# A hybrid decoder trunk on one core: the recurrence's banks are emptied right behind their products, and four due times are moved

## The chip, the cores and the metric

The kernel runs on one core of a Trainium2 chip, as one launch. The metric is the device time of that launch in microseconds (us), as the median of several runs. A profiled execution of the same program gives the trace from which all shorter times here are read. The engines are named as the profile names them: PE (TensorE, the matmuls; PEld its weight loads), DVE (VectorE), ACT (ScalarE), POOL (GpSimd) and SP (SyncE, which issues most DMAs).

## The reference

The program computes two decoder layers on x of 1024 tokens by 1024 columns, in float32. Layer 0 mixes tokens by a gated linear recurrence (HGRN2), layer 1 by sliding-window attention; each is followed by a gated convolution FFN. The change touches the recurrence and the way into layer 0's FFN:

```python
q, f, i, g = jnp.split(h @ w_in, 4, axis=-1)          # w_in: (1024, 4096), 8 heads of 128
fg = lb + (1.0 - lb) * jax.nn.sigmoid(heads(f))
o = hgrn2_chunkwise(jax.nn.silu(heads(q)), 1.0 - fg, heads(i), jnp.log(fg))
# S_t = diag(f_t) S_{t-1} + k_t v_t^T ; o_t = S_t^T q_t
o = o * lax.rsqrt(jnp.mean(jnp.square(o), -1, keepdims=True) + RMS_EPS)
o = o * g_norm_w * jax.nn.silu(heads(g))
mix = o.reshape(B, S, D) @ w_out
h = layer_norm(ALPHA * h + mix, ln_mix_g, ln_mix_b)
u = h @ ffn_w_in          # (1024, 5632), then conv of width 3, silu gate, @ ffn_w_out
```

## The kernel before, in words

**Matmuls.** Every large matmul is done to nearly float32 accuracy from operands split into a high part (cast on ACT) and a low part (the rest, subtracted on DVE: `low_part`, L197). `mm3` (L222 to L224) issues three matmuls of 128x128 by 128x512: high by high, high by low, low by high. Four such groups make a *product*, 12 matmuls.

**The recurrence's line of products.** The projections q, f (which makes the gates and keys), i (values) and g (output gate) are done head by head. Head 0's come first, in the plain way. For heads 1 to 7 the projections go in pairs: pair m = 2(h-1) is (f, q) of head h, pair m + 1 is (i, g). Each pair is done by seven products p = 1 to 7 on sums of blocks (a Strassen-Winograd scheme: the tokens' halves against the halves of the 1024 inputs). `line` lists the 98 products of all pairs in the order of PE: (m,1), (m-1,3), (m-1,4), (m,6), (m,5), (m,2), (m,7), and so on; the first pair has 1, 2, 6, 5, 7 in a row. The four x operands of these products are T, and TXs[0] to TXs[2] with the sums of x's blocks, made by `sums_of_x` and `last_sums`. The fourth product, (0,5), reads the last part of T that `last_sums` fills (cast L874, low part L197); the code finishes `last_sums` right before it.

**Banks.** The products share four PSUM banks (`product`, L1401). Product 2 has bank 1, products 5 and 3 have bank 2, and 1, 6, 7, 4 of pair m add up in bank 0 or 3, by m's parity. Product 6 adds onto what product 1 left, 7 onto 6, and 4 onto 7, so a product may not start before the bank's last content has been read. That reading is `evacuate` (L1367): a copy on ACT for products 1, 6, 5 and 4 (L1378 to L1387), an add on DVE for 2, 7 and 3 (L1390), and behind the add a gate on ACT (`forget`, L1013, or Silu). `readers[b]` holds the evacuation of bank b, so that the next product on b can see to it that it has been issued.

**Weights.** `job_next` (L1304 on) makes the products' weights in the order of `jobs`: sums "a" and "b" of a pair (two DVE operations each, L1315 and L1316, L1318 and L1319) and one low part per product (DVE, L197), behind a cast of the high part (`cast_next`, ACT, L1296). The low part of product 4 of a pair also issues the loads of two raw weight tiles for the pairs to come (SP). `ensure(n)` (L1356) forces these jobs until the product at place n of the line has its weights; `product(n)` calls it for n + 2. Weights lie in a ring of eight slots (`home`).

**The order.** Inside this stage PE, SP, ACT, DVE and POOL do their instructions in the order in which the code issues them. `Order` (L55) plans that order by hand: `od.t` is the planned time of PE, advanced with each matmul issued, and `od.v` the planned end of DVE's work, advanced by `od.vec`. A task (`od.spawn(gen, delay)`) is a generator that issues some instructions, yields the time until its next step is due, and is stepped by `od.tick()`, which is called behind each group of three matmuls. A tick steps the tasks that are due, then issues casts that are ready (`hook`), then fills DVE with jobs (`fill`) as long as `od.v` is less than 0.5 us ahead of `od.t`. `od.behind(us, least)` (L72) is the time until DVE's planned end plus `us`, and at least `least`. So an evacuation spawned with a delay of 0.3 was issued at the first tick of the next product: behind the `ensure` at that product's start and behind tasks due earlier.

**A head's recurrence.** `recur` (L1044 on) is a task too: elementwise products and updates on DVE (L1114 to L1119), copies of their results on ACT (`stash`, L1101, L1102), small matmuls of 32 rows for the sums and scores on PE (L228), and so on; near its end it turns the values' tile on PE (for heads from 1 on), copies it back on ACT (L1194), waits a due time of 1.3 us and multiplies keys by values (L228). `all_heads` does one head after the other and waits between them until the next head's gates are there. `values` (L753) empties a block of head 0's values and gates: copy (ACT, L756), add (DVE, L758), and behind every second block a Silu of two blocks (ACT, L765), due 0.7 us behind the add's issue.

**The entry of a layer.** `ffn` calls `out_proj` (L356 on): the mixer's output projection in two halves of the columns, eight token blocks each; in the second half the blocks come as 4, 5, 6, 7, 0, 1, 2, 3, and behind each block its `Up.ln` (L418) is spawned: the layer norm on DVE (`ln_affine`, L280, L283), and some us of matmuls later its turn: 8 transposes on PE (L232) into two banks of the same pool of four that `out_proj` uses, split into T by ACT and DVE. That due time was 10.0 for blocks 4 to 7 and 8.0 for blocks 0 to 3, in both layers. `Up.run` then does the up-projection by seven products of its own. Outside the recurrence and the attention only PE's order is the code's; the other engines are ordered by a scheduler, and the code between `urgent()` goes first.

Of the kernel before, what the change touches and what calls it, by code (L numbers as in the profile page):

```python
# [22 lines left out]
NH = 8  # L23
# [111 lines left out]
def trunk(ctx: ExitStack, tc: tile.TileContext, a: dict, out: bass.AP):  # L135
    nc = tc.nc
    PS = bass.MemoryType.PSUM
    od = Order()
# [29 lines left out]
    def psmm():  # L168
        return mmp.tile([P, 512], F32, name="psmm")

    def psax():
        return axp.tile([P, 1024], F32, name="psax")

    def urgent():

        return tc.high_priority(offset=300)
# [54 lines left out]
    def tr(ps, src):  # L231
        nc.tensor.transpose(ps, src, ident)  # L232
        od.t += 0.109
# [14 lines left out]
    def split(hi, lo, src, eng=None):  # L248
        nc.scalar.copy(hi, src)  # L249
        return low_part(lo, src, hi, eng)  # L250
# [8 lines left out]
    def ln_half(tb, i):  # L259

        if tb not in half_stats:
            half_stats[tb] = sm.tile([P, 2, 6], F32, name="st", bufs=8)
        nc.vector.bn_stats(half_stats[tb][:, i, :], Y[:, tb, i * 512:(i + 1) * 512])  # L263
# [10 lines left out]
    def ln_affine(tb, rows, dst, n=1):  # L274

        y = Y[:, tb, :]
        mv, rs = ln_stats(tb)
        parts = [slice(h * D // n, (h + 1) * D // n) for h in range(n)]
        for hs in parts:
            nc.vector.scalar_tensor_tensor(y[:, hs], y[:, hs], mv[:, 0:1], rows[0][:, hs],  # L280
                                           op0=ALU.subtract, op1=ALU.mult)
        for hs in parts:
            nc.vector.scalar_tensor_tensor(y[:, hs], y[:, hs], rs, rows[1][:, hs], op0=ALU.mult, op1=ALU.add)  # L283
            nc.sync.dma_start(dst(hs), y[:, hs])
# [118 lines left out]
    class Up:  # L403
# [14 lines left out]
        def ln(self, tb):  # L418
            with urgent():
                ln_affine(tb, self.rows, lambda hs: ynd[:, tb, hs], 2 if tb == 3 else 1)  # L420
            yield 10.0 if tb > 3 else 8.0
            turned = lambda t: (self.rx[2 * t - 4] if t in (2, 3) else Y[:, t, :]).rearrange("p (k t) -> p k t", k=KC)
            hf = turned(tb)
            ts = slice(tb * P, (tb + 1) * P)
            with urgent():
                for q in range(2):
                    ps, ks = psmm(), slice(4 * q, 4 * q + 4)
                    for k in range(4):
                        tr(ps[:, k * P:(k + 1) * P], Y[:, tb, (4 * q + k) * P:(4 * q + k + 1) * P])
                    pv = ps.rearrange("p (k t) -> p k t", k=4)  # L430
                    if tb < 4:
                        split(T[:, 0, ks, ts], T[:, 1, ks, ts], pv)
                        nc.scalar.copy(hf[:, ks], pv)
                    elif q == 0:
                        nc.scalar.copy(hf[:, ks], pv)
                    else:
                        split(T[:, 0, ks, ts], T[:, 1, ks, ts], pv)
                        tt(hf[:, ks], hf[:, :4], pv, op=add)
                        split(T[:, 0, :4, ts], T[:, 1, :4, ts], hf[:, ks])
                        return  # L440
            sf = turned(tb + 4)
            a11, a12, a21, s1 = hf[:, :4], hf[:, 4:], sf[:, :4], sf[:, 4:]
            tt(a21, a11, a21, op=sub)
            tt(a11, s1, a11, op=sub)
            tt(a12, a12, a11, op=sub)
            split(self.T2[:, 0, :, ts], self.T2[:, 1, :, ts], a21)
            yield 100.0
            pair = hf.rearrange("p (c k) t -> p c k t", c=2)
            split(self.TX[:, :, 0, :, ts], self.TX[:, :, 1, :, ts], pair)
# [37 lines left out]
        def product(self, p, fc, ps):  # L487
            TX = self.TX
            moving = {1: lambda j, k: T[:, j, k, :512], 2: lambda j, k: T[:, j, 4 + k, :512],
                      3: lambda j, k: TX[:, 1, j, k, :], 4: lambda j, k: T[:, j, 4 + k, 512:],  # L490
                      5: lambda j, k: T[:, j, k, 512:], 6: lambda j, k: TX[:, 0, j, k, :],
                      7: lambda j, k: self.T2[:, j, k, :]}[p]
            block = {1: 0, 2: 1, 5: 2, 4: 3, 7: 4, 6: 5, 3: 6}[p]
            ws = self.W[fc]
            fixed = lambda j, k: (ws[6][:, 512 * j + 128 * k:512 * j + 128 * k + 128] if block == 6 else
                                  ws[block // 2 * 2 + j][:, 512 * (block % 2) + 128 * k:512 * (block % 2) + 128 * k + 128])
            for k in range(4):
                mm3(ps, lambda j: fixed(j, k), lambda j: moving(j, k), k == 0, k == 3)
                od.tick()
            return ps  # L500
# [84 lines left out]
    class Down:  # L585
# [70 lines left out]
        def evacuate(self, p, tb, ps, ln):  # L656
            lo, hi = [Y[:, t, :].rearrange("p (h n) -> p h n", h=2) for t in (tb, tb + 4)]
            c11, c12, c21, c22 = lo[:, 0], lo[:, 1], hi[:, 0], hi[:, 1]
            plus, minus = {1: ([c11, c21], [c12, c22]), 2: ([c11], []), 5: ([c12, c22], []), 6: ([c21], [c22, c12]),
                           7: ([c22], [c21]), 3: ([c12], []), 4: ([c21], [])}[p]  # L660
            for y, op in [(y, add) for y in plus] + [(y, sub) for y in minus]:
                if p == 1:
                    nc.vector.scalar_tensor_tensor(y, y, ALPHA, ps, op0=ALU.mult, op1=op)
                else:
                    tt(y, y, ps, op=op)

            if p in (2, 3, 4, 7):
                ln_half(tb if p in (2, 3) else tb + 4, 0 if p in (2, 4) else 1)
            if p in (3, 4):
                task = ln(tb if p == 3 else tb + 4, self)  # L670
                if task is not None:
                    self.tasks.append(od.spawn(task))
# [51 lines left out]
    with tc.tile_pool(name="t", bufs=1, reuse_waits="tile") as raws, hgrn_pool as hp:  # L724
# [28 lines left out]
        def values(tb, ps):  # L753

            vg = VG[0][:, :, tb * P:(tb + 1) * P]
            nc.scalar.copy(vg, ps[:, 256:].rearrange("p (g c) -> p g c", g=2))  # L756
            yield 0.9
            nc.vector.tensor_tensor(vg, vg, ps[:, :256].rearrange("p (g c) -> p g c", g=2), op=ALU.add)  # L758
            od.vec(0.45)
            if tb == NB - 1:  # L760
                values_in[0] = 0
            if tb % 2:
                G = VG[0][:, 1, (tb - 1) * P:(tb + 1) * P]
                yield 0.7
                nc.scalar.activation(G, G, AF.Silu)  # L765

        def first_values(ps):
# [276 lines left out]
        def recur(h, qs, fg, kp):  # L1044
# [96 lines left out]
            ps = psax()  # L1141
# [37 lines left out]
            ps = psax()  # L1179
# [10 lines left out]
            if h:  # L1190
                ps = psax()
                for c in range(NB):
                    tr(ps[:, c * P:(c + 1) * P], V[:, c, :])
                nc.scalar.copy(VG[h][:, 0, :], ps)  # L1194
                yield 1.3
            ps = psax()
            for c in range(NB - 1):
                cs = slice(c * P, (c + 1) * P)
# [12 lines left out]
            ps = psax()  # L1211
# [45 lines left out]
        line = [(0, 1), (0, 2), (0, 6), (0, 5), (0, 7)]  # L1257
# [20 lines left out]
        def home(n):  # L1278
            return HL[:, n % 8, :].rearrange("p (h n) -> p h n", h=2)
# [76 lines left out]
        def ensure(n):  # L1356
            while line[n] not in low_made:
                if not job_next(True):
                    raise ValueError("a weight block is not made")
# [5 lines left out]
        targets, readers, evacs = {}, {}, {}  # L1365
# [35 lines left out]
        def product(n):  # L1401

            m, p = line[n]
            ensure(min(n + 2, len(line) - 1))
            b = {2: 1, 5: 2, 3: 2}.get(p, 3 * (m % 2))
            ps = banks[b]
            if b in readers:
                t, taken = readers[b]
                while not taken:
                    od.step(t)  # L1410
            w = home(n)
            for k in range(4):
                od.t += 0.031
                mm3(ps, lambda j: w[:, j, k * P:(k + 1) * P], lambda j: moving[p](j, k), k == 0 and p in (1, 2, 5), k == 3, onto=p in (6, 7, 3, 4))
                od.tick()
            done[0] = n + 1
            taken = []
            readers[b] = od.spawn(evacuate(m, p, ps, taken), 0.3), taken
            evacs.setdefault(m, []).append(readers[b][0])

        values_done, normed = [-1], []
        wo = a["hgrn_w_out"][0]
# [42 lines left out]
        with tc.manual_schedule(engines={EN.PE, EN.SP, EN.Activation, EN.DVE, EN.Pool}):  # L1465
# [27 lines left out]
            for n, (m, p) in enumerate(line):  # L1493
# [3 lines left out]
                h, g = pairs[m]  # L1497
# [55 lines left out]
        ps = psax()  # L1553
# [26 lines left out]
    with (tc.tile_pool(name="ta", bufs=1, reuse_waits="tile") as raws,  # L1580
# [190 lines left out]
        with tc.manual_schedule(engines={EN.PE, EN.Activation, EN.DVE, EN.Pool}):  # L1771
# [34 lines left out]
            for c in range(8):  # L1806
                fill = q_proj(hl) if c < 7 else last_filler()
                nq, nd = next(fill)
                for bp in range(0, 4, 2):
                    n = 2 * c + bp // 2  # L1810
# [49 lines left out]
            for _ in range(2):  # L1860
                ps = psax()
# [49 lines left out]
```

## Time and profile before

| | |
|---|---|
| median of 3 runs | 2125.34 us (2123.89 to 2126.57) |
| profiled execution, whole | 2124.68 us |
| profiled execution, span from first to last instruction | 2122.8 us |
| mean granted clock of TensorE | 0.997 |
| the line of 98 products | from 63.2 to about 442.5 us of the span |
| DVE busy, ACT busy | 84%, 45% of the span |

Lines of the profile name the engine, the line of the code, what is written and what is read. In a timeline the first two numbers are the start and the length in us, and a bracket at the end gives how long the engine stood idle before, and whose end it waited for. In the list of waits the numbers are the total in us, how many times, and the longest. In a table by stage, each engine has its busy time and its number of instructions; the last three numbers are the granted clock of TensorE, the busy share of the DMA engines, and GB/s.

### The profile page before, as it was taken

The page shows a single profiled execution, that of the slowest core. Times are in us where ns is not written, and L with a number is a line of the kernel's source. Part 1 is how long each engine was busy: PE and PEld are TensorE (multiplying, and loading weights), DVE is VectorE, ACT ScalarE, POOL GpSimd, SP SyncE. Part 2 cuts the span into 40 slices and gives each one's busy share as a digit, 9 for nine tenths or more (in the row PEclk, how much of TensorE's full clock was granted, in tenths as well). Part 3 has the DMA queues.
Part 4 walks back from the last instruction along what each step waited for, and adds up shares of the span by engine and source line. Part 5 has one row for each costly group of instructions (what it writes and reads, how often), then busy time and mean ns, then how long its engine had stood idle before and what let it go on. Part 6 is the DMA issues. An engine that isn't in the chain of part 4 may idle for free. (4 is left out here: it accounts for less than half of the span.)

```text
span 2122.8 us, 31567 instructions
## 1 busy us (share of the span) xinstructions
PE 2093.4 (99%) x12303; PEld 1740.8 (82%) x12303; DVE 1777.7 (84%) x2420; ACT 965.2 (45%) x1562; POOL 187.2 (9%) x214
## 2 busy tenths in 40 slices
PE   9899999999999999999999999999999999999998
PEld 8687888887888888888888888888888888888887
DVE  6677777768999999988988768969999999978986
ACT  6454555542444344434433267743544444444430
POOL 1000000001110000100001122321010000000002
PEclk9999999999999999999999999999999999999999
DMA  4011111253237766628854511042266776449662
GB/s 153 21 51 51 51 51 52 63 190 100 90 117 182 178 167 161 159 91 293 276 189 159 159 33 38 23 149 95 85 170 168 178 171 164 122 149 328 224 206 99
DMA packets 239823, 286.81 MB, mean 135 GB/s; under 512 B 30217, under 2 KB 160441, under 8 KB 239417
## 3 DMA queue, kind: packets, MB, share of 16 engines
q1 hardware_dynamic: 223360, 238.26, 34.7%
q0 software_dynamic: 15456, 46.16, 10.9%
q8 instruction: 97, 1.59, 0.3%
q14 instruction: 54, 0.43, 0.1%
q10 hardware_dynamic: 856, 0.37, 0.1%
HBM read 241.72 MB, written 89.15 MB: 156 GB/s over the span
## 5 line engine op out<-in xcount | busy, mean ns | idle before, releaser
L222 PE MATMUL psmm<-T,HL 128*128 128x512 f32 x816 | 323.1, 396 | 6.9 <-ACT T L874 3.6
L223 PE MATMUL psmm<-T,HL 128*128 128x512 f32 x816 | 319.0, 391 | 1.7 <-DVE T L197 1.7
L224 PE MATMUL psmm<-T,HL 128*128 128x512 f32 x816 | 319.2, 391 | 0.3 <-DVE HL L197 0.2
L528 DVE SCALAR_TENSOR_TENSOR Y<-Y,cwt,Y 128x1023 f32<-128x1023 f32 (+1 forms) x176 | 225.2, 1281 | 49.6 <-ACT Y L526 48.3
L249 ACT CAST HL<-rx 128x1024 fp32r<-128x1024 f32 (+1 forms) x151 | 150.8, 1005 | 149.8 <-DMA rx<-in_ffn_w_in_dram 33.1
L197 DVE TENSOR_TENSOR HL<-rx,HL 128x1024 fp32r<-128x1024 f32 (+1 forms) x151 | 180.1, 1198 | 14.9 <-ACT HL L249 14.5
L222 PEld LDWEIGHTS psmm<-T,HL 128*128 128x128 f32 x816 | 153.8, 188 | 38.9 <-ACT T L874 4.1
L224 PEld LDWEIGHTS psmm<-T,HL 128*128 128x128 f32 x816 | 153.7, 188 | 33.6 <-DVE HL L197 1.2
L223 PEld LDWEIGHTS psmm<-T,HL 128*128 128x128 f32 x816 | 153.9, 189 | 33.3 <-DVE T L197 2.7
L222 PE MATMUL psax<-T,HL 128*128 128x512 f32 x392 | 153.2, 391 | 1.3 <-DVE Y L513 0.9
L224 PE MATMUL psax<-T,HL 128*128 128x512 f32 x392 | 152.6, 389 | 0.0
L223 PE MATMUL psax<-T,HL 128*128 128x512 f32 x392 | 152.5, 389 | 0.0
L526 ACT ACTIVATE Y<-Y,cwt 128x1024 f32<-128x1024 f32 x88 | 108.8, 1237 | 91.9 <-DVE Y L515 80.5
L197 DVE TENSOR_TENSOR HL<-raw,HL 128x512 fp32r<-128x512 f32 (+1 forms) x121 | 92.7, 788 | 43.2 <-ACT HL L1296 33.5
L271 POOL TENSOR_TENSOR rs<-rs,nhalf 128x1 f32<-128x1 f32 x32 | 45.6, 1425 | 735.1 <-DVE rs L270 731.1
L249 ACT CAST HT<-rx 128x1024 fp32r<-128x1024 f32 (+1 forms) x37 | 35.5, 960 | 146.1 <-DVE rx L482 62.0
L222 PEld LDWEIGHTS psax<-T,HL 128*128 128x128 f32 x392 | 73.6, 188 | 17.6 <-DVE Y L513 1.3
L222 PE MATMUL psmm<-HL 128*128 128x512 f32 x220 | 86.5, 393 | 0.0
L224 PEld LDWEIGHTS psax<-T,HL 128*128 128x128 f32 x392 | 73.6, 188 | 15.4
L223 PEld LDWEIGHTS psax<-T,HL 128*128 128x128 f32 x392 | 73.6, 188 | 15.0
L224 PE MATMUL psmm<-HL 128*128 128x512 f32 x220 | 85.7, 390 | 0.0
L223 PE MATMUL psmm<-HL 128*128 128x512 f32 x220 | 85.6, 389 | 0.0
(404 smaller groups left out, 5197.1 us busy)
## 6 DMA issues: line engine op xcount, KB each, us to landing
rx<-in_ffn_w_in_dram SPq DMA_DIRECT2D x136, 256.0 KB
rx<-gd SPq DMA_DIRECT2D x118, 256.0 KB
bsd<-in_ffn_w_out_dram POOLq DMA_DIRECT2D x36, 768.0 KB, 8.6
gd<-Y SPq DMA_DIRECT2D x44, 512.0 KB
raw<-in_hgrn_w_in_dram SPq DMA_DIRECT2D x30, 512.0 KB
rx<-in_ffn_w_out_dram SPq DMA_DIRECT2D x54, 256.0 KB
R<-bsd SPq DMA_DIRECT2D x44, 256.0 KB
Y<-in_ffn_w_in_dram SPq DMA_DIRECT2D x40, 256.0 KB
```

The costliest lines, as they stand in the source:

```text
L197: make = lambda e: e.tensor_tensor(lo, src, hi.bitcast(F32), op=ALU.subtract)
L222: nc.tensor.matmul(ps, st(0), mv(0), start=start, stop=False, skip_group_check=onto)
L223: nc.tensor.matmul(ps, st(0), mv(1), start=False, stop=False, skip_group_check=onto)
L224: nc.tensor.matmul(ps, st(1), mv(0), start=False, stop=stop, skip_group_check=onto)
L249: nc.scalar.copy(hi, src)
L271: nc.gpsimd.tensor_tensor(rs, rs, nhalf, op=ALU.pow)
L526: nc.scalar.activation(c, u, AF.Identity, bias=cwt[:, l, 3, ci:ci + 1], scale=cwt[:, l, 2, ci:ci + 1])
L528: nc.vector.scalar_tensor_tensor(c[:, sh:], u[:, :S - sh], cwt[:, l, 2 - sh, ci:ci + 1], c[:, sh:], op0=ALU.mult, op1=ALU.add)
```

## The change

Five edits. (1) `product` steps the evacuation's task itself, as soon as the product's matmuls have been issued, so that its first instruction (copy or add) is issued there; it is no longer issued at the first tick of the next product. (2) `product(n)` asks for the weights of product n + 3, not n + 2. (3) The Silu of head 0's gates in `values` is due 0.1 us behind DVE's planned end, and at least 0.7. (4) In `recur`, the products of keys by values are due 2.2 us behind the copy of the turned values, not 1.3, for heads 1 to 5; heads 6 and 7 keep 1.3. (5) In layer 0, the turns of blocks 4 to 7 are due 13.0 us behind their layer norm, not 10.0; blocks 0 to 3 keep 8.0, and layer 1 keeps 10.0 and 8.0. No instruction is added or left out.

```diff
@@ -418,7 +418,7 @@
         def ln(self, tb):
             with urgent():
                 ln_affine(tb, self.rows, lambda hs: ynd[:, tb, hs], 2 if tb == 3 else 1)
-            yield 10.0 if tb > 3 else 8.0
+            yield 8.0 if tb < 4 else 10.0 if self.l else 13.0
@@ -761,7 +761,7 @@
             if tb % 2:
                 G = VG[0][:, 1, (tb - 1) * P:(tb + 1) * P]
-                yield 0.7
+                yield od.behind(0.1, 0.7)
                 nc.scalar.activation(G, G, AF.Silu)
@@ -1192,7 +1192,7 @@
                 nc.scalar.copy(VG[h][:, 0, :], ps)
-                yield 1.3
+                yield 2.2 if h < NH - 2 else 1.3
@@ -1401,7 +1401,7 @@
             m, p = line[n]
-            ensure(min(n + 2, len(line) - 1))
+            ensure(min(n + 3, len(line) - 1))
@@ -1415,8 +1415,9 @@
             done[0] = n + 1
             taken = []
-            readers[b] = od.spawn(evacuate(m, p, ps, taken), 0.3), taken
+            readers[b] = od.spawn(evacuate(m, p, ps, taken)), taken
             evacs.setdefault(m, []).append(readers[b][0])
+            od.step(readers[b][0])
```

## Prediction, made before the changed kernel was run

> **What bounds the kernel now.** I read the page first, then PE's waits, then timelines around the longest of them, then the table by stage.
>
> ```profile
> span 2122.8 us, 31567 instructions
> PE 2093.4 (99%) x12303; PEld 1740.8 (82%) x12303; DVE 1777.7 (84%) x2420; ACT 965.2 (45%) x1562; POOL 187.2 (9%) x214
> ```
>
> PE sets the time: it is idle for about 29 us of 2122.8. No arithmetic is taken away by this change, so all it can win is idle time of PE, or time at a lower clock. The profiled execution took 2124.68 us, 1.9 us more than its span and 0.7 us less than the median of the runs, 2125.34. Next: who keeps PE waiting, from 60 to 480 us (us in total, times, longest), and two rows of the same view over 0 to 620 us.
>
> ```profile
> PE psmm L222 <- ACT T L874: 3.6, 1, 3.6
> PE psmm L222 <- DVE VG L1390: 2.8, 1, 2.8
> PE psax L228 <- ACT VG L1194: 2.6, 5, 0.7
> PE psmm L222 <- ACT fg L1378: 1.8, 1, 1.8
> PE psmm L223 <- DVE T L197: 0.9, 1, 0.9
> ...
> PE psmm L232 <- DVE Y L283: 2.0, 1, 2.0
> PE psmm L224 <- DVE HL L197: 0.2, 1, 0.2
> ```
>
> Together 13.9 us, and each of these waits stands where the change has an edit. A row understates its loss: a matmul of 512 columns is shown busy for 0.39 us, but the next one starts 0.23 us behind it, so each wait costs 0.16 us more than its idle time.
>
> **Evacuation first, at 188 us.** The add that empties bank 2 is L1390; DVE, then PE:
>
> ```profile
> 184.70 0.71 DVE L1318 TENSOR_TENSOR raw<-raw 128x512 f32<-128x512 f32 x1
> 185.44 0.69 DVE L1319 TENSOR_TENSOR raw<-raw,raw 128x512 f32<-128x512 f32 x1
> 186.82 0.69 DVE L197 TENSOR_TENSOR HL<-raw,HL 128x512 fp32r<-128x512 f32 x1 [0.68 <-ACT HL L1296]
> 187.43 0.68 DVE L1390 TENSOR_TENSOR VG<-VG,psmm 128x512 f32<-128x512 f32 x1
> ```
>
> ```profile
> 185.06 0.39 PE L224 MATMUL psmm<-Y,HL 128*128 128x512 f32 x1
> 188.25 0.47 PE L222 MATMUL psmm<-T,HL 128*128 128x512 f32 x1 [2.81 <-DVE VG L1390]
> ```
>
> PE could have gone on at 185.06 + 0.23 = 185.29 and went on at 188.25: 2.96 us lost. Ahead of the add stand the two sums and the low part that ensure() forces, and DVE's own 0.68 us wait for the cast between them. These are issued in the next product, ahead of the evacuation, whose task is due 0.3 us later. The change issues the evacuation as soon as its product's matmuls are issued, so the add starts where the first sum did, 184.70, and ends at 185.4: PE waits 0.1 to 0.2 us, a gain of 2.8. Three products ahead, the sums are also forced a product earlier, which may push the recurrence's step that DVE did before them behind the add; then all 2.96 go. I take **2.8** (2.3 if DVE lags by another operation, to 2.96).
>
> The edit adds no instruction. Where an engine reaches the evacuation before PE has finished the product, what is queued behind it waits too: forced sums and low parts on DVE, casts on ACT, and the products that use them. They are for products two or three later, at 2.72 us each (12 matmuls of 0.23), which covers it; without cover a product would lose at most one low part and one cast, 0.69 us and a quarter of 2.17 (a row below). I take 0.
>
> **Weights three products ahead.** The same sums and low parts, 2.72 us earlier; two weight loads on SP behind the low part of product 4 go ahead with it, and their tiles still wait for the last cast that reads them. The wait at a low part (0.2 idle, 0.36 lost) goes: **0.3**. Against it, up to four DVE operations (two sums, two low parts, 4 x 0.6 us at the pace above) now stand ahead of an update of the recurrence that they used to follow. Its consumer, PE's small matmuls, is issued at DVE's planned end plus 0.6 us, so it moves back by whole matmul groups (0.68 us) instead of waiting; heads 2 to 5 wait for the next head's gates, so there it costs nothing.
>
> **Values' gate later, and the first products.** ACT, then PE:
>
> ```profile
> 63.51 0.42 ACT L765 ACTIVATE VG<-VG 128x256 f32<-128x256 f32 x1 [5.96 <-DVE VG L758]
> 63.83 0.35 ACT L756 COPY VG<-psmm 128x256 f32<-128x256 f32 x1
> ...
> 68.09 2.17 ACT L1296 CAST HL<-raw 128x512 fp32r<-128x512 f32 x4
> 70.17 0.58 ACT L1378 COPY fg<-psmm 128x512 f32<-128x512 f32 x1
> ```
>
> ```profile
> 68.56 0.39 PE L224 MATMUL psmm<-T,HL 128*128 128x512 f32 x1
> 70.80 0.50 PE L222 MATMUL psmm<-Y,HL 128*128 128x512 f32 x1 [1.85 <-ACT fg L1378]
> ...
> 77.51 0.39 PE L224 MATMUL psmm<-Y,HL 128*128 128x512 f32 x1
> 81.53 0.79 PE L222 MATMUL psmm<-T,HL 128*128 128x512 f32 x1 [3.64 <-ACT T L874]
> 83.18 0.79 PE L223 MATMUL psmm<-T,HL 128*128 128x512 f32 x1 [0.86 <-DVE T L197]
> ```
>
> The gate at 63.51 held ACT for 5.96 us, with the next block's copy (63.83) behind it; DVE in turn waited for that copy. With the gate due behind DVE's planned end, the copy is done long before, and the chain copy, add, update, ACT's copies, last gate and casts up to the evacuation at 70.17 comes about 0.8 us earlier. The evacuation keeps its place there, since no other ACT work was issued between. So the third product starts at about 70.0 instead of 70.80.
>
> The fourth product waits for the last quarter of x's sums in T. Its chain starts when the recurrence's scores leave PE:
>
> ```profile
> 76.38 0.69 DVE L1114 TENSOR_TENSOR qp<-qp,tot 128x512 f32<-128x512 f32 x1 [4.31 <-PE psax L228]
> ...
> 81.22 1.91 DVE L197 TENSOR_TENSOR T<-VG,T 128x512 fp32r<-128x512 f32 x3
> ```
>
> From 76.38 to the last low part's end, 83.13, are 6.75 us that the change leaves as they are. (The evacuation of the third product, 0.58 us on ACT, now stands ahead of the last cast; that delays the fourth product's first matmul, not the second, which waits for DVE.) But the scores move back by one group of three matmuls, 0.68 us, since a low part is forced ahead of the update before them. At equal clock 0.8 - 0.7 leaves nothing. The clock decides (PEclk is the column behind the engines):
>
> ```profile
> 67.92:71.33 3.41, 1.56 (x7) 1.01 (x6) 2.47 (x5) 3.35 (x7) 0.00 (x0) 1.00 0.00 0
> 71.33:74.74 3.41, 3.41 (x25) 1.98 (x27) 0.74 (x2) 0.00 (x0) 0.00 (x0) 0.50 0.00 0
> ...
> 81.57:88.40 6.83, 5.97 (x13) 4.37 (x14) 2.76 (x5) 0.51 (x2) 0.00 (x0) 0.50 0.46 131
> 183.97:187.38 3.41, 1.48 (x7) 0.90 (x5) 2.65 (x5) 1.21 (x3) 0.00 (x0) 1.00 0.00 0
> ```
>
> In the stretch behind the 1.85 us wait the granted clock is 0.50 for 3.41 us, behind the next for 6.83 us. Half of 3.41 is 1.7 us lost. With the wait cut from 2.01 lost (70.80 - 68.56 - 0.23) to 1.2, PE is busy for over half of the 3.41 us, and I expect full clock; then the scores leave 1.7 + 0.1 = 1.8 us earlier, and so does the fourth product. The second spell stays, as the wait before it gets longer (about 6 us); it may end a stretch earlier. I take **2.0** for both; bounds -0.3 (spell stays, one group later) and 3.5 (both shorten by a stretch). The Trainium skill ("TensorE: Matmul & The Clock Gate", "Why this matters for your kernels") asks for idle gaps of over some 3 us before the clock halves. The trace disagrees: 1.85 us was enough here, while 2.81 us at 188 left the clock at 1.00. By that rule the shorter gap would change no clock and this term would be about 0, the time 2 us longer.
>
> **Products later behind the values' turns.**
>
> ```profile
> 151.85 0.39 PE L224 MATMUL psmm<-T,HL 128*128 128x512 f32 x1
> ...
> 152.95 0.41 PEld L228 LDWEIGHTS psax<-VG,kd 128*128 128x128 f32 x3 [1.13 <-ACT VG L1194]
> ```
>
> PE comes to the values 0.87 us too early here, while ACT copies the turned values (152.95 - 151.85 - 0.23). Five such waits make 2.6 + 5 x 0.16 = 3.4. With 2.2 for 1.3, and issue points every 0.68 us, two more groups (1.36 us) lie between, which covers 0.87 with 0.5 to spare, for heads 1 to 5, all five. If a forced cast stands ahead of the copy on ACT, up to 0.6 comes back in some. I take **3.2** (2.3 to 3.4).
>
> **First entry's turns later.**
>
> ```profile
> 516.71 1.09 PE L232 MATMUL psmm<-ident,Y 128*128 128x128 f32 x8 [1.99 <-DVE Y L283]
> ```
>
> ```profile
> 500.00:573.00 73.00, 71.01 (x344) 58.70 (x344) 70.61 (x109) 31.14 (x48) 11.80 (x8) 1.00 0.27 96
> ```
>
> 3 us of matmuls more ahead of the first turn cover the 2.15 us lost. But DVE is busy 70.61 of 73 us there, so PE's lead can be given back where PE next waits for DVE. And block 0 comes one product (24 matmuls, 5.4 us) behind block 7: its turn, due after 8, stood 3 us behind block 7's, due after 10; with 13 they meet in one product, so four turned halves and the running product want five banks of a pool of four; the last waits for an ACT copy or a DVE operation, 0.6 to 1.3 us by the rows above. I take **1.2** (-0.5 to 2.15).
>
> **The sum.** 2.8 + 0.3 + 2.0 + 3.2 + 1.2 = 9.5; 0.5 off for small waits that a new order of 98 products brings somewhere, the size of the smallest rows above. 2124.7 - 9.0 = 2115.7, and with the 0.7 us by which the median stood higher 2116.4. All good ends make 12.3 (2113), all bad ones with 3 us of new waits 1.1 (2124).
>
> **Rivals.** *The gains of the first products and of the first entry don't come* (clock stays at 0.50, DVE takes back the turns): for it, DVE's 70.61 of 73 and the spells that I can't date; 2.8 + 0.3 + 3.2 - 0.5 = 5.8, so 2119.6 (2118.4 if the clock alone stays). By the Trainium skill's rule above that last case is the likely one; the row of 0.50 behind 1.85 us speaks against it, and I leave it a third of this rival's chance. *The waits move on*: a bank or a cast is late elsewhere by 0.7 us or so per head, 5 us over seven, against a gain of 5 to 9; 2121 to 2125, no change. For it, DVE was 3 us behind PE at 188; against it, DVE stands idle for a sixth of the span. *Slower*: the forced group of four (2.4 us) stands ahead of the update in each of seven heads, and PE reaches the scores before it, because real DVE lags its plan by more than the 0.6 us margin: 7 x 2.4 = 17 less 9, 2133. It decides from 1.3 us a head on. Against it: no PE wait in the list is for DVE's qp or kp, so the margin holds with the groups of today.
>
> **How the numbers follow.** A measurement of this kernel can tell about 0.2%, 4.25 us, from no change: the bound is 2121.1. Forecast 0.66 (2113 to 2119), first rival 0.21, second 0.08, slower 0.05. Range 2112 to 2121.5: it takes in the first rival and the bounds of the first products. The forecast and the first rival lie below the bound: faster 0.87, same 0.08, slower 0.05.
>
> **What would show it.** Right: PE's waits for VG L1390, for L1194 in heads 1 to 5 and for Y L283 are gone; the gate L765 no longer holds ACT for 6 us; clock 1.00 behind the third product's start, and still 0.50 behind the fourth's. Wrong: PE waits for qp, kp or psmm at turn 0; a spell of 0.50 at 71 us as before; longer waits at 600 us and later.

## The result, and the profile after

The changed kernel takes 2121.69 us (median, 2118.18 to 2122.29), beside 2126.85 us for the kernel before on the same chip: a ratio of 0.9975, interval 0.9966 to 0.9984. It is faster, but by 5.2 us where 9 were forecast, and 0.2 us outside the range. The profiled execution took 2122.24 us, its span 2120.4.

The page after, its first two lines of figures:

```profile
span 2120.4 us, 31566 instructions
...
PE 2091.9 (99%) x12303; PEld 1742.8 (82%) x12303; DVE 1777.2 (84%) x2420; ACT 968.1 (46%) x1562; POOL 187.1 (9%) x214
```

PE is idle for 28.5 us of its span; before it was 29.4. So almost as much idle time is left as there was, in other places. PE's waits over the whole span (us in total, times, longest), the rows that matter:

```profile
PE psmm L222 <- ACT T L874: 4.8, 1, 4.8
PE psmm L224 <- DVE HL L197: 2.9, 2, 2.7
PE psmm L232 <- DVE Y L380: 1.6, 1, 1.6
...
PE psmm L232 <- ACT Y L433: 1.2, 1, 1.2
...
PE psmm L222 <- ACT fg L1378: 1.0, 1, 1.0
...
PE psmm L232 <- DVE Y L438: 0.4, 1, 0.4
...
PE psax L228 <- ACT VG L1194: 0.4, 1, 0.4
...
PE psmm L232 <- ACT Y L435: 0.2, 1, 0.2
```

The wait for VG L1390 is gone, the one for L1194 fell from 2.6 us in five to 0.4 in one, the third product's from 1.8 to 1.0. The fourth product's (T L874) is longer, as the prediction said, since PE comes to it earlier. At the first entry's turns (L232) one wait of 2.0 became four with 3.4 in all, and a wait of 2.7 for a low part of the weights (HL L197) is new.

Where the recurrence ends, the same turn of the last heads' output, first in the kernel before and then in the changed one (start, us, engine and line):

```profile
480.87 1.03 PE L232 MATMUL psax<-ident,og 128*128 128x128 f32 x8
```

```profile
473.94 1.03 PE L232 MATMUL psax<-ident,og 128*128 128x128 f32 x8
```

6.9 us are won here, although this execution was 0.47 us late before the first product, ahead of every edit:

```profile
63.19 0.50 PE L222 MATMUL psmm<-T,HL 128*128 128x512 f32 x1 [0.41 <-DVE VG L758]
```

```profile
63.66 0.49 PE L222 MATMUL psmm<-T,HL 128*128 128x512 f32 x1 [0.41 <-DVE VG L758]
```

So the recurrence gave 7.4 us (forecast: 8.3 for its four terms, less 0.5). At the end of the span 2.4 are left. The loss lies in the first entry, at its turns and near 612 us. By the same matmuls in both profiles, PE's lead of 6.9 us falls to 5.2 over the turns (557.23 for 562.45), and from 6.4 to 1.8 at 612 (606.18 for 612.60, then 621.68 for 623.48): behind the wait of 2.68 us the clock is halved for 3.41 us (613.29 to 616.70), which costs 1.7 more. PE, POOL, ACT and DVE after:

```profile
516.00 0.60 PE L232 MATMUL psmm<-ident,Y 128*128 128x128 f32 x4
518.24 0.66 PE L232 MATMUL psmm<-ident,Y 128*128 128x128 f32 x4 [1.64 <-DVE Y L380]
...
539.97 0.66 PE L232 MATMUL psmm<-ident,Y 128*128 128x128 f32 x4 [1.16 <-ACT Y L433]
...
612.20 0.50 PE L224 MATMUL psmm<-TX,HL 128*128 128x512 f32 x1 [2.68 <-DVE HL L197]
```

```profile
593.27 3.77 POOL L533 TENSOR_TENSOR Y<-Y 128x1024 f32<-128x1024 f32 x1 [42.85 <-DVE Y L528]
```

```profile
597.07 1.25 ACT L526 ACTIVATE Y<-Y,cwt 128x1024 f32<-128x1024 f32 x1 [3.35 <-POOL Y L533]
```

```profile
516.31 1.27 DVE L283 SCALAR_TENSOR_TENSOR Y<-Y,rs,rx 128x1024 f32<-128x1024 f32 x1
517.50 0.68 DVE L380 SCALAR_TENSOR_TENSOR Y<-Y,psmm 128x512 f32<-128x512 f32 x1
...
594.71 0.68 DVE L511 TENSOR_TENSOR Y<-Y,psax 128x512 f32<-128x512 f32 x1
598.35 1.28 DVE L528 SCALAR_TENSOR_TENSOR Y<-Y,cwt,Y 128x1023 f32<-128x1023 f32 x1 [2.97 <-ACT Y L526]
...
601.94 2.62 DVE L482 TENSOR_TENSOR Y<-Y,rx 128x512 f32<-128x512 f32 x1
...
610.94 1.21 DVE L197 TENSOR_TENSOR HL<-Y,HL 128x1024 fp32r<-128x1024 f32 x1
```

At 516.00 a block's first half (x4) finds a bank, its second half none: the bank is emptied by the output product's add (L380), and DVE comes to that add at 517.50, behind a block's normalization (L283) and weight sums. Behind 594.71 DVE runs into a convolution step (L528) whose input ACT can write (L526) only when POOL's product of 3.77 us has read the tile: 2.97 us of standing still, with the weight sum L482 and the low parts queued behind. The last of these, at 610.94, is what PE waits for at 612.20. Before, the sum stood ahead of the step that waits, and the wait was 0.23:

```profile
600.61 0.68 DVE L482 TENSOR_TENSOR Y<-Y,rx 128x512 f32<-128x512 f32 x1
...
607.81 1.28 DVE L528 SCALAR_TENSOR_TENSOR Y<-Y,cwt,Y 128x1023 f32<-128x1023 f32 x1 [0.23 <-ACT Y L526]
```

The table by stage over the same window as before shows how full each engine is (PE, PEld, DVE, ACT, POOL busy):

```profile
500.00:573.00 73.00, 69.52 (x337) 57.55 (x336) 70.63 (x109) 31.13 (x48) 11.20 (x8) 1.00 0.29 101
```

DVE is busy for 70.63 us of 73, as before (70.61); PE does 1.5 us less in them.

### The profile page after: what moved, and what is told of

The parts are those of the page before. It is cut to its first block, busy times and chain, and to the rows that moved or that the text cites. A ratio compares the mean times of both kernels' runs of the same rounds, so it can differ in the third digit from the quotient of the medians.

```text
span 2120.4 us, 31566 instructions
## 1 busy us (share of the span) xinstructions
PE 2091.9 (99%) x12303; PEld 1742.8 (82%) x12303; DVE 1777.2 (84%) x2420; ACT 968.1 (46%) x1562; POOL 187.1 (9%) x214
## 5 line engine op out<-in xcount | busy, mean ns | idle before, releaser
L528 DVE SCALAR_TENSOR_TENSOR Y<-Y,cwt,Y 128x1023 f32<-128x1023 f32 (+1 forms) x176 | 225.1, 1281 | 49.7 <-ACT Y L526 48.3
L197 DVE TENSOR_TENSOR HL<-rx,HL 128x1024 fp32r<-128x1024 f32 (+1 forms) x151 | 176.4, 1175 | 17.6 <-ACT HL L249 17.3
L526 ACT ACTIVATE Y<-Y,cwt 128x1024 f32<-128x1024 f32 x88 | 108.8, 1237 | 92.8 <-DVE Y L515 82.8
L197 DVE TENSOR_TENSOR HL<-raw,HL 128x512 fp32r<-128x512 f32 (+1 forms) x121 | 92.2, 789 | 40.6 <-ACT HL L1296 30.7
```

What stands on the lines that cost most here:

```text
L197: make = lambda e: e.tensor_tensor(lo, src, hi.bitcast(F32), op=ALU.subtract)
L526: nc.scalar.activation(c, u, AF.Identity, bias=cwt[:, l, 3, ci:ci + 1], scale=cwt[:, l, 2, ci:ci + 1])
L528: nc.vector.scalar_tensor_tensor(c[:, sh:], u[:, :S - sh], cwt[:, l, 2 - sh, ci:ci + 1], c[:, sh:], op0=ALU.mult, op1=ALU.add)
```

## The experiments

Fourteen kernels, each beside the kernel before on the same chip. The medians come from several chips, on which the kernel before took 2125.85 to 2126.85 us, so versions of different chips are compared more safely by the ratio:

| version | median us | ratio to before | interval |
|---|---|---|---|
| changed kernel | 2121.69 | 0.9975 | 0.9966 to 0.9984 |
| e1 changed, turns as before | 2116.81 | 0.9961 | 0.9949 to 0.9973 |
| e2 before, turns alone | 2129.57 | 1.0016 | 1.0007 to 1.0024 |
| e3 changed, only the first turn later | 2116.31 | 0.9956 | 0.9944 to 0.9968 |
| e4 = e1, gate as before | 2120.70 | 0.9976 | 0.9967 to 0.9986 |
| e5 before, values alone | 2133.51 | 1.0033 | 1.0021 to 1.0046 |
| e6 before, evacuation alone | 2126.22 | 1.0003 | 0.9994 to 1.0012 |
| e7 before, weights alone | 2127.59 | 1.0008 | 0.9999 to 1.0017 |
| e8 = e1, evacuation as before | 2120.72 | 0.9975 | 0.9967 to 0.9984 |
| e9 = e1, weights as before | 2132.43 | 1.0028 | 1.0016 to 1.0039 |
| e10 = e1, values as before | 2122.74 | 0.9989 | 0.9980 to 0.9998 |
| f1 changed, L533 on VectorE | 2116.44 | 0.9949 | 0.9937 to 0.9962 |
| f4 changed, no weight sums in groups 0, 1 | 2117.93 | 0.9962 | 0.9949 to 0.9976 |
| f5 = e3, L533 on VectorE | 2115.78 | 0.9951 | 0.9937 to 0.9965 |
| f7 before, L533 on VectorE | 2125.62 | 0.9997 | 0.9988 to 1.0006 |

### The first entry's turns: e1, e2, e3

e1 undoes the edit, e3 keeps it for one block; e2 puts e1's minus line into the kernel before as its only edit.

```diff
-            yield 8.0 if tb < 4 else 10.0 if self.l else 13.0
+            yield 10.0 if tb > 3 else 8.0
```

```diff
-            yield 8.0 if tb < 4 else 10.0 if self.l else 13.0
+            yield 8.0 if tb < 4 else 13.0 if tb == 4 and not self.l else 10.0
```

> The changed kernel with the turns' due time of layer 0 back at 10.0; the other four edits stay. Theory 'turns' (the later turns lose behind the recurrence what was won in it): the recurrence keeps its 8 us, the entry of layer 0 is as before (one wait of 2.0 us at the first turn, no 2.7 us wait and no spell of clock 0.50 near 612 us), so about 8 us faster than the kernel before, 2118 to 2119. Theory 'lead' (PE arrives 8 us earlier at a DVE that is full, whatever the turns): the waits behind 500 us are as in the changed kernel, and the time stays at 2121 to 2122.

> The kernel before with the turns of blocks 4 to 7 in layer 0 at 13.0, nothing else. Theory 'turns': slower than before by 2 to 5 us, 2129 to 2132, with PE waiting for banks at the turns (4 us in all instead of 2) and a long wait near 620 us. Theory 'lead': the turns alone win their 1 to 2 us, 2125.

> The changed kernel with 13.0 for block 4 alone, blocks 5 to 7 back at 10.0. If it is the crowding of turns 5, 7 and 0 and out_proj's banks that costs, the 2.0 us wait of the first turn is won without it: 2116 to 2117. If DVE's work sets the pace from 505 to 570 us, the wait comes back at the next turn: 2118 to 2119, as with 10.0 for all.

The edit alone makes the kernel before 3.7 us slower by medians (3.4 by the ratio), and without it the changed kernel reaches 2116.81, close to the forecast for all five edits and below what either theory of e1 gave. e2 shows the changed kernel's waits one by one, with none of the recurrence's edits; PE's waits of e2 from 500 to 700 us:

```profile
PE psmm L224 <- DVE HL L197: 2.7, 1, 2.7
PE psmm L232 <- DVE Y L380: 1.7, 1, 1.7
PE psmm L232 <- ACT Y L433: 1.2, 1, 1.2
PE psmm L232 <- DVE Y L438: 0.4, 1, 0.4
PE psmm L232 <- ACT Y L435: 0.2, 1, 0.2
```

So the loss belongs to this edit: in e2's profile PE is 2.6 us behind the kernel before where the recurrence ends (483.43 for 480.87) and 6.4 at the end of the span (2129.2 for 2122.8), 3.8 more. In e1 the first turn waits 2.7 us; in e3 no turn waits over 0.6, but a wait of 1.2 for L507 comes at 632 us, where e1 had 0.7 and 1.1. The two times cannot be told apart; it looks as if what is saved at the turns is asked for later.

### What makes the first entry wait: f4, f1, f5, f7

f4 leaves out eight sums that the program needs, so that only its time counts: eight operations less on DVE, with PE's order in this stage the same; f1 takes POOL's product out of the chain. f5 is f1's edit on e3, f7 on the kernel before.

```diff
+            if self.l or fc > 1:
+                for o, x, y in ((b11, b12, b11), (b12, b22, b12), (b22, b22, b11), (b21, b21, b22)):
+                    tt(o, x, y, op=sub)
-            tt(b11, b12, b11, op=sub)
-            tt(b12, b22, b12, op=sub)
-            tt(b22, b22, b11, op=sub)
-            tt(b21, b21, b22, op=sub)
```

```diff
-                    (nc.gpsimd if fc < 2 else nc.vector).tensor_tensor(ca, ca, c, op=ALU.mult)
+                    nc.vector.tensor_tensor(ca, ca, c, op=ALU.mult)
```

> The changed kernel without the four differences of the weight blocks (L480 to L483) of groups 0 and 1 in the first entry: these sums are left out, 8 VectorE operations at 0.60 us, 4.8 us of its work between 505 and 612 us; TensorE's order is the same. Theory 1 (VectorE's work sets the pace of the first entry, and a later due time of the turns only moves the place of the wait): the waits at the turns (3.5 us in four) fall to under 1.8 and the one at 612 to under 1, time 2115.5 to 2118.5. Theory 2 (the turns wait for banks because their due times put too many half blocks into one product, whatever VectorE has to do): at least 3 us of the turns' waits stay and only what hangs on the weight sums at 612 changes, time 2118.5 to 2122.

> The changed kernel with the feed-forward's gate product of groups 0 and 1 (L533) on VectorE instead of GpSimd, in every layer. Theory 1 (the 2.68 us wait at 612 us comes from the order: VectorE stands 2.97 us for an activation that waits for GpSimd's 3.77 us product, with the weight sums and low parts queued behind it): the wait at 612 and the half clock behind it go, and the time falls by 2 to 4.5 below the changed kernel's, 2117 to 2119.5, or a little less if the other entries' two more VectorE operations of 1.2 us cost something. Theory 2 (VectorE is behind by its whole work since the turns, whatever stands ahead): 2.4 us more work of VectorE make the wait at about 612 as long or longer, and the time is 2121 to 2124.

> The version with only block 4's turn later (2116.3) and the products L533 on VectorE. Theory: the first entry then has neither bank waits at the turns (3.4 us in the changed kernel, 1.4 in this base) nor the stall that GpSimd's product brings near 600 to 640 us (the base waits 1.2 us at L507): 2113.5 to 2115.5. Rival: VectorE sets the pace from 505 to 640 us anyway, its two more operations (2.4 us) are paid at a later wait: 2116 to 2117.5.

> The kernel before with the products L533 on VectorE alone. Theory 1 (GpSimd's product costs only where VectorE's order puts the weight sums behind the operation that waits for it, which the late turns brought about): waits of 0.9 and 0.4 at 609 and 640 us go at most, ratio 0.9985 to 0.9998. Theory 2 (GpSimd's product costs as much whatever the turns): 4 us or more are won here too, ratio under 0.998.

PE's waits from 480 us on, f4 and then f1, all rows:

```profile
PE psmm L224 <- DVE HL L197: 3.0, 1, 3.0
PE psax L222 <- DVE Y L518: 0.4, 1, 0.4
```

```profile
PE psmm L232 <- DVE Y L380: 1.6, 1, 1.6
PE psmm L232 <- ACT Y L433: 1.2, 1, 1.2
PE psmm L232 <- DVE Y L438: 0.4, 1, 0.4
PE psmm L232 <- ACT Y L435: 0.2, 1, 0.2
```

These two separate the causes. With 4.8 us less work for DVE all four waits at the turns are gone, though the due times put the same half blocks into the same products: the crowd of turns alone makes no wait, DVE's work must keep the banks as well (theory 1 for the turns). The wait at 612 us stays at 3.0 all the same, so here both theories of f4 missed. It goes when POOL's product goes, with two DVE operations more (theory 1 of f1): it comes from the order in which DVE meets the step that waits for POOL. f1 also removes an add that POOL's product slows (L482, 2.62 us), but the kernel before has such slowed operations too (L197, 2.83 us for 1.22 and 2.61 for 0.68) and no such wait; what is new is DVE's stand of 2.97 us, found in the changed kernel, e2, f4 and e9, the four profiles with the long wait at this place. f1 is 0.0026 of the time below the changed kernel (0.9975 to 0.9949), 5.5 us, more than its theory said; its edit also acts in the other entries.

f7 wins nothing clear of noise, as its theory 1 said: the waits of 0.9 and 0.4 go, and one of 1.1 for a low part comes. So POOL's product costs much only in the unlucky order. That late turns alone bring this order about is refuted by e9 below: with the turns as before DVE stands the same 2.97 us ahead of L528, and PE 3.1. f5 wins nothing over e3 or f1; its gain was forecast too large, and waits of 1.5 and three of 0.6 follow up to 650 us. The medians of e1, e3, f1 and f5 lie within about 1 us of each other, their ratios in each other's intervals, 3 to 5.5 us below the changed kernel's.

### The recurrence's edits one at a time: e4 to e10

e5, e6 and e7 make one edit of the change.diff in the kernel before; e4, e8, e9 and e10 undo one in e1. The edits, each as the change has it:

```diff
-                yield 0.7
+                yield od.behind(0.1, 0.7)
...
-                yield 1.3
+                yield 2.2 if h < NH - 2 else 1.3
...
-            ensure(min(n + 2, len(line) - 1))
+            ensure(min(n + 3, len(line) - 1))
...
-            readers[b] = od.spawn(evacuate(m, p, ps, taken), 0.3), taken
+            readers[b] = od.spawn(evacuate(m, p, ps, taken)), taken
+            od.step(readers[b][0])
```

> As the first kernel of this batch (turns at 10.0), and the Silu of head 0's gates back at 0.7 us behind its add. My theory of the first products: the third product starts 0.8 us later, its wait is 1.8 us again, and the clock falls to 0.50 for 3.4 us behind it in most executions: 2 us slower than the first kernel of this batch, 2120 to 2121. Rival: the clock does not hang on this wait, 0 to 0.8 us slower.

> The kernel before with 2.2 for 1.3 behind the values' turns alone. Theory of the term (3.2): PE's waits for L1194 (2.6 us in five) fall to at most 0.5 us in all, the later course is unchanged, and the time falls by 3.0 to 3.4: ratio to before 0.9984 to 0.9986. Rival: the 1.4 us of matmuls moved ahead of the values are missing elsewhere in the head, a wait of 0.3 or more per head appears at another line, and less than 1.5 us is won: ratio over 0.9993.

> The kernel before with the evacuation's first step issued straight behind its product, nothing else. Theory of the term (2.8): PE's wait for L1390 at 188 us falls from 2.81 to under 0.4 and no other wait over 0.5 us appears ahead of 500 us; 2.3 to 2.96 us less: ratio 0.9986 to 0.9989. Rival: the add itself goes first, but forced sums and casts behind it make a product late, a new wait at L197 or L249 of 1 us or more, and the gain is under 1.5 us: ratio over 0.9993.

> The kernel before with the weights three products ahead, nothing else. Theory 1 (what kept VectorE from the add at 188 us were the sums forced in that product; forced a product earlier, they leave the add where it can go, whatever the evacuation's due time): the wait for L1390 falls from 2.8 to under 0.5 us with this edit alone, ratio 0.9975 to 0.9988. Theory 2 (as the prediction split it: 2.8 us by the evacuation's place, 0.3 by this edit): the wait of 2.8 stays, ratio 0.9995 to 1.0005.

> The changed kernel with the turns' due times of before and with the evacuation due 0.3 us behind its product as before; weights three ahead, gate and values as changed. Its base (turns as before) took 2116.8. Theory 1 (the edits interlock: with the products moved behind the values' turns, or with sums forced a product earlier, the late adds L1390 stop PE several times): waits for L1390 and L1380 of 5 us or more in all between 180 and 410 us, time 2121 to 2127. Theory 2 (the terms add up as in the prediction): one wait of about 2.8 at 188 us, time 2119 to 2120.

> The changed kernel with the turns' due times of before and the weights two products ahead as before; evacuation first, gate and values as changed. Theory 1 (interlock: the evacuation that goes first pushes the forced sums, low parts and casts behind it, and two products do not cover them): a wait for the cast L1296 of about 2 us near 188 us, as with the evacuation alone, time 2118.3 to 2120. Theory 2 (terms add up): the wait of 0.2 at a low part comes back and nothing else, time 2116.8 to 2117.3.

> The changed kernel with the turns' due times of before and the values' turns covered by 1.3 us of products as before; evacuation first, weights three ahead and gate as changed. Its base took 2116.8. Theory 1 (the term of 3.2 us holds where the weights are three ahead): waits for L1194 of 2 us or more in all come back, time 2119.5 to 2121. Theory 2 (weights three ahead already change where the products lie, and the 2.2 only pays for itself in part): under 1.2 us of waits for L1194, time 2116.8 to 2118.5.

None of the three wins alone. Taken out of e1, each edit costs, by the ratios, 3.2 us for the gate (which was not tried alone), 3.0 for the evacuation, 6.0 for the values and 14.2 for the weights (by medians 3.9, 3.9, 5.9 and 15.6). For the gate and the evacuation the intervals overlap e1's, so these two prices are the least sure. The profiles show where they fall: the turn of the last heads, at 472.44 us in e1, comes 1.8 us later in e4, 2.3 in e8, 4.7 in e10 and 14.1 in e9. The rest of e4's and e8's price lies behind the recurrence. The terms of the sum are not a property of the edits one by one.

**Evacuation alone (e6).** DVE and PE of e6, then ACT and PE of the same pattern in e9:

```profile
183.09 0.72 DVE L1390 TENSOR_TENSOR VG<-VG,psmm 128x512 f32<-128x512 f32 x1
183.72 0.68 DVE L1318 TENSOR_TENSOR raw<-raw 128x512 f32<-128x512 f32 x1
```

```profile
185.83 0.50 PE L222 MATMUL psmm<-T,HL 128*128 128x512 f32 x1 [1.99 <-ACT HL L1296]
```

```profile
183.15 2.70 ACT L1296 CAST HL<-raw 128x512 fp32r<-128x512 f32 x5 [4.98 <-DVE raw L1319]
...
183.82 0.50 PE L222 MATMUL psmm<-T,HL 128*128 128x512 f32 x1 [1.99 <-ACT HL L1296]
```

The add goes first as meant, but the sums behind it make the cast late for the very next product: 2.81 us of waiting become 1.99. The rival was right, at another line than it named. In e9 this happens in three heads (6.0 us in all), and the 2.7 us wait for L1390 comes back in a fourth. Behind each of these four waits the clock is halved for 3.41 us, 6.8 us lost in all; with that e9's 2132.43 lies far above both its theories, which ended at 2120.

**Weights alone (e7).** The stall at 188 us is gone with the evacuation's due time of before: the sums start at 176.76, the add follows at 180.66, and PE has no wait between 160 and 200 us. Theory 1 named the mechanism; neither named the time, since the gain is given back at the values:

```profile
151.49 1.13 ACT L1296 CAST HL<-raw 128x512 fp32r<-128x512 f32 x2
152.52 1.01 ACT L1194 COPY VG<-psax 128x1024 f32<-128x1024 f32 x1
...
153.58 1.83 PE L228 MATMUL psax<-VG,kd 128*128 128x128 f32 x14 [1.74 <-ACT VG L1194]
```

Casts forced a product earlier stand ahead of the copy on ACT (first two rows), and PE waits 1.74 at this head; the waits for L1194 grow from 2.6 to 4.1. That is what the 2.2 us of products cover: without them the rest has 3.7 us there (e10, as its theory 1 said, at a time 1.7 us above that theory's).

**Values alone (e5).** The waits for L1194 are all gone, as expected, and 8.4 us for L1390 in three come for them. DVE and PE at the second of these:

```profile
290.21 0.71 DVE L1318 TENSOR_TENSOR raw<-raw 128x512 f32<-128x512 f32 x1
290.95 0.69 DVE L1319 TENSOR_TENSOR raw<-raw,raw 128x512 f32<-128x512 f32 x1
292.33 0.69 DVE L197 TENSOR_TENSOR HL<-raw,HL 128x512 fp32r<-128x512 f32 x1 [0.68 <-ACT HL L1296]
292.94 0.68 DVE L1390 TENSOR_TENSOR VG<-VG,psmm 128x512 f32<-128x512 f32 x1
```

```profile
293.76 0.77 PE L222 MATMUL psmm<-T,HL 128*128 128x512 f32 x1 [2.79 <-DVE VG L1390]
```

It is the sequence of 188 us before, now in more heads. That the products moved behind the values are missing as cover for the forced sums is the likely reason; with weights three ahead (e8) none of these waits is left. The edit does what it says at its place, and the time goes 7 us the other way, further than its rival said.

**Without the evacuation (e8).** No wait for L1390 comes back at all, against both theories; there are waits of 0.9 at kd L1185, 1.2 in two at L1194 and 3.1 at the first turn (0.2, 0.4 and 2.7 in e1). Its price is spread over small waits and one stretch of 3.41 us at half clock at 512 us, and no single row carries it.

**Gate as before (e4).** The third product waits 1.89 us again. Only ACT's order differs from e1. The time, 2120.70, is the one that its theory gave, but by another way: in the profile no half clock follows the third product. The recurrence ends 1.8 us later than in e1, about the forecast term; the rest is lost at a first turn of 3.5 us with 6.83 us at half clock behind it, at 510 us, in a stage that the gate is not part of.

## Why the prediction was wrong

**The step that failed** is "3 us of matmuls more ahead of the first turn cover the 2.15 us lost ... I take 1.2 (-0.5 to 2.15)". It measured a loss of 3.7 us (e2; 1.5 to 5.1 by its interval), outside its own bounds. These 4.9 us too many are more than the whole forecast is off by (9.0 against 5.2): the other four edits gave 9.0 by medians (e1), 1.2 above their 7.8 with the 0.5 taken off, and 9.0 - 3.7 is about the 5.2 that was measured. The cover itself came, since no wait for Y L283 is left. What the step set against it fell short in two parts:

- "DVE takes back the turns" stood in the text with its row (70.61 of 73 us), but with a price of the lead alone. The meeting of turns was priced at one wait of 0.6 to 1.3 us; it came as four, 3.4 us. f4 showed that the meeting makes no wait without DVE's weight sums among the operations that empty the banks.
- The prediction followed the turns and not what their DVE operations push past. DVE's order in this stage is a scheduler's, and with the later turns it put the weight sums behind a convolution step that waits for POOL. f1 showed this for the 2.7 us at 612, which cost 4.6 with the half clock behind them. "longer waits at 600 us and later" was named as a sign of being wrong, but got no term.

The other signs of being right came: no wait for L1390, one of 0.4 us for L1194, no wait of over 0.2 us ahead of the gate L765, and the clock as said behind the third and the fourth product.

**The recurrence's sum** held (7.4 and, in e1's profile, 8.4 at the same turn, for 7.8), its split did not. 2.8 for the evacuation and 0.3 for the weights are the wrong way round: e7 removes the stall with the weights alone, e6 only swaps it for a cast. "They are for products two or three later ... which covers it" failed where they are two ahead: 1.99 us, not nothing and not the 1.2 at most. That the sum came out all the same is in part luck: the change happens to contain the cover that each edit needs from the others.

**Values' turns: 3.2.** The waits fell by 2.2 of 2.6 us; as part of the set the edit is worth 5.9 (e10): it also covers what the earlier casts cost (3.3 us of waits for L1194 between e10 and e1).

**First products: 2.0.** The wait fell by 0.84 us, forecast 0.8. The third product ran at full clock, the fourth waited longer, and its spell of half clock stayed:

```profile
80.81:87.63 6.82, 6.43 (x14) 4.68 (x15) 1.05 (x2) 0.99 (x2) 0.00 (x0) 0.50 0.00 0
```

The fourth product started 0.78 us earlier than before (81.53 to 80.75), 1.25 with the late start taken off, and its first low part's wait fell from 0.86 to 0.39. One product on (90.86 before) 1.5 us are won here (89.82, late start taken off) and 2.5 in e1 (88.32), whose first products are the same but whose spell begins at 78.12: the 2.0 lies between, and how much is won depends on where the spell falls.

**The rivals.** "The waits move on" forecast 2121 to 2125, where the result lies, but in the recurrence and at 0.7 us a head, which did not happen. They did move on, one stage later. That the first entry's gain does not come was a rival at 2119.6 together with the clock; that it turns into a loss of over 0.5 us was in no case.

## What to carry to other kernels

When an engine is busy for 97% of a stage, moving its consumer later may buy nothing in that stage (e3 against e1), and each new due time can reorder what stands behind it; look for the operation in that queue that waits for a slow third engine. Edits to one pipeline (how far ahead weights are made, who empties a bank first, how much work covers a turn) are to be priced as a set: each can win nothing alone and be worth 3 us or more in its place, here up to 14. Where a planner orders the queues, undoing each edit in the finished version told more here than trying each on the old one, and an edit in another stage should be timed by itself.

## What the runs showed of the hardware

From 60 us to the end of the first entry the half clock comes in stretches on a fixed grid: each lasts 3.41 or 6.83 us, and starts lie a whole number of 3.413 us apart (80.81 and 613.29 in the changed kernel: 532.48, 156 times). PE's busy time within the stretch before decides, as far as these profiles show. Changed kernel, then e4 at its third product (PE busy is the first number behind the length; the clock stands after the engines):

```profile
609.87:613.29 3.42, 1.09 (x5) 0.91 (x6) 3.42 (x5) 2.65 (x4) 0.00 (x0) 1.00 0.24 70
613.29:616.70 3.41, 3.41 (x10) 2.67 (x9) 3.41 (x5) 1.04 (x1) 0.00 (x0) 0.50 0.79 236
```

```profile
66.92:70.33 3.41, 1.79 (x8) 1.14 (x7) 1.89 (x4) 3.27 (x7) 0.00 (x0) 1.00 0.00 0
70.33:73.74 3.41, 3.14 (x29) 2.25 (x33) 3.31 (x7) 0.74 (x2) 0.00 (x0) 1.00 0.00 0
```

e4 waited 1.89 us and kept its clock: its wait reached past the end of the stretch, which was left with 1.79 us busy. The kernel before waited 1.85 with 1.56 us busy, and its clock was halved. Over the profiles of this case, from 66 to 660 us, a stretch at full clock with under 1.35 us busy was always followed by half clock and one with over 1.7 never; from 1.42 to 1.56 it went both ways (10 times half, 4 times full). So the 2.81 us wait at 188 kept the clock at 1.00 in the profile of before (1.48 busy in its stretch), and halved it for 6.83 us in e2 (1.43 busy) and in f7 (1.32), whose code is the same up to there; e2:

```profile
184.28:187.69 3.41, 1.43 (x7) 0.85 (x5) 2.66 (x6) 1.26 (x3) 0.00 (x0) 1.00 0.00 0
187.69:194.52 6.83, 6.01 (x105) 4.74 (x106) 3.77 (x9) 3.61 (x8) 0.00 (x0) 0.50 0.01 2
```

A stall that PE runs into can therefore cost 1.7 or 3.4 us more (half of 3.41 and of 6.83) by where it lies among the stretches, which differs between executions and after any earlier edit. The Trainium skill ("TensorE: Matmul & The Clock Gate", "Why this matters for your kernels") puts the limit at idle gaps of over some 3 us; by the rows above a gap of 1.85 us can be enough and one of 2.81 us need not be.

An add on VectorE that takes 0.68 us elsewhere took 2.62 us while GpSimd ran its product beside it (L482 at 601.94; POOL's second L533 from 601.60, 2.41 us), and ended 0.55 us behind it. At 593.57 it went the other way: a low part of VectorE kept its 1.22 us, and POOL's product, begun at 593.27, took 3.77 us.
